# A two-layer hybrid trunk in float32: attention and scan products in fuller rows and in turn, and other work at the two ends

## The chip, the cores and the metric

The kernel runs on one core of a Trainium2 chip. The metric is the device time of one execution in microseconds; the time before is the median of three runs. One more execution was taken with the hardware profiler, and all rows below are from it. The engines are named as in the profile: PE is TensorE (PEld its weight loads), DVE is VectorE, ACT is ScalarE, POOL is GpSimd, and SP issues DMAs.

## The reference

Two layers over 256 tokens of width 2048, in float32. The even layer runs a Mamba-2 scan (SSD, 16 heads of 64) beside block attention (MoBA, 8 heads of 128; at this length each query sees its one block). The odd layer runs NSA (three attention branches, 8 query heads over 2 key heads) beside retention. Each layer then has an output projection, a norm, a gated convolutional FFN and a norm.

```python
def even(h):
    z, xbc, dt, q, k, v = split(h @ w_in)
    y_diag = einsum('bgcls,bghcls,bcsghp->bclghp', cb, decay, xdt_g)   # SSD, one chunk of 256
    o = softmax(q @ k.T * scale + rel_bias, causal) @ v                # MoBA
def odd(h):
    q, kc, vc, ks, vs, kw, vw, gates, rq, rk, rv, rg = split(h @ w_in)
    k_cmp, v_cmp = compress(kc), compress(vc)          # 15 blocks of 32 tokens, stride 16
    o = g0 * attend(q, k_cmp, v_cmp) + g1 * attend(q, ks, vs) + g2 * attend(q, kw, vw)
x = LN(alpha * x + concat(groups) @ w_out)
x = LN(alpha * x + (silu(conv(a)) * u) @ w_down)       # a, u = split(x @ w_up)
```

The relative bias is a table of 32 buckets by 8 heads, spread over distances.

## The kernel before

**Weights.** All weights stream from HBM in slabs of 128 rows. `Weights.prep` (lines 97 to 110) loads a slab into one of four `wraw` buffers, ScalarE rounds it to `whi` (108) and VectorE takes the rest into `wlo` (109); four buffers each. Activations are split in the same way, so that a projection is three fast products per slab: `three` (350 to 355) where the tokens are stationary, and line 314 in `group_b` where the weights are. Products in plain float32 (attention, scan, transposes by a product with the identity) appear in the trace as two records each, transposes as one. SP issues the loads in order; a load waits for its `wraw` buffer, and so for the conversion of four slabs earlier, and that for the products of four slabs earlier.

**Start.** `warm_up` (1151 to 1158) multiplies ones by ones 20 times while the first data arrive. `run` (1160 to 1180) loads x in eight pieces of 256 KB and pumps weight slabs between them, then loads constants and the residual rows `r` (2 MB), and then makes the bias row: `bias_scratch` (558 to 571) multiplies the table by a one-hot matrix (568) and writes the result to DRAM, from where `load_bias` reads it back for each layer. The first group of the even layer (`group_a`, lines 373 to 396) has 16 slabs of 696 columns in two accumulators, the second eight slabs of 688.

**Order.** Small work (SSD, attention, retention) is cut into steps and put into `Fill`; the projection loops pop one step every few products, so that small products stand between large ones. The framework then orders each engine's queue.

**SSD.** `diag(ct)` (839 to 855) makes the output of two heads, each on 64 of 128 columns of the array, with three products a head: first all of one head, then all of the other.

**Attention.** `attn_steps` (599 to 676) gives three steps per head. `scores` multiplies q by k in two parts, as the mask is causal (first 128 queries by 128 keys, the other 128 by 256), into one PSUM tile `S`, then takes the softmax (584 to 593; VectorE adds the bias and takes the minimum, ScalarE the exponential). NSA adds two products with the compressed keys, of 7 and of 15 columns (615, 616). `normalise` scales and transposes by `ident` (639; compressed 652, 653). `mix` (659 to 674) multiplies by the values: per half of the queries and per branch, so three products in MoBA and eight in NSA, of which two have 7 and 15 rows. `pair` puts two heads' steps side by side. `compress` (1002 to 1042) makes the compressed keys and values; its `project` for the values makes two products (1038).

**The last norm.** `out_group` of the last FFN (`idx` 3) finishes the first 128 tokens, then the last six slabs for the other 128; `Norm.start` (194 to 219) then takes mean and variance, GpSimd raises to the power of -0.5 (199), and VectorE makes two passes over each of four column blocks (`first`, `second`) with a store after each. The order there is kept as it is written.

Of the kernel before, what the change touches and what calls it, by code (L numbers as in the profile page):

```python
# [28 lines left out]
WARM = 20  # L29
# [130 lines left out]
class Norm:  # L160
# [33 lines left out]
    def start(self, t):  # L194
# [38 lines left out]
    def store(self, t, at, n):  # L233
        cs = slice(at, at + n)
        self.k.nc.sync.dma_start(self.k.out[128 * t:128 * t + 128, cs], self.k.r[:, t, cs])
# [25 lines left out]
class Trunk:  # L261
# [111 lines left out]
    def group_a(self, act, *evacs, widths=None, early=None):  # L373
# [7 lines left out]
        for s in range(head, KT // m):  # L381
            hi, lo = w.get(first + s)
            for kk in range(m):
                k = m * s + kk
                c = 0
                for n, acc, evac in zip(widths, accs, evacs):
# [171 lines left out]
    def bias_scratch(self):  # L558

        nc = self.nc  # L560
        self.scr = self.dram.tile([8, 384], F32, name="scr")
        with self.tc.tile_pool(name="bias0", bufs=1) as P:
            oh = P.tile([32, 384], F32, name="oh")
            nc.sync.dma_start(oh, self.I["c_onehot"])
            mk = P.tile([8, 384], F32, name="mk")
            nc.sync.dma_start(mk, self.I["c_late"])
            ps = self.ps()
            nc.tensor.matmul(ps[:8, :384], self.rel[:32, :], oh, start=True, stop=True)
            vv = P.tile([8, 384], F32, name="vv")
            nc.vector.scalar_tensor_tensor(vv, ps[:8, :384], -1.0 / SCALE, mk, op0=OP.mult, op1=OP.add)  # L570
            nc.sync.dma_start(self.scr, vv)
# [12 lines left out]
    def softmax(self, P, S, nb0, nb1, w0, w1, z, stat, j):  # L584
# [3 lines left out]
        for i, (c, n, nb) in enumerate(((0, w0, nb0), (w0, w1, nb1))):  # L588
            nc.vector.tensor_tensor_reduce(out=z[:, c:c + n], in0=S[:, c:c + n], in1=nb, scale=SCALE, scalar=3e38,
                                           op0=OP.add, op1=OP.min, accum_out=mn[:, i:i + 1])  # L590
        for i, (c, n) in enumerate(((0, w0), (w0, w1))):
            nc.scalar.activation(z[:, c:c + n], z[:, c:c + n], AF.Exp, scale=-1.0, bias=mn[:, i:i + 1],
                                 accum_out=stat[:, j + i:j + i + 1])
# [5 lines left out]
    def attn_steps(self, P, y, ct, h, branches, gate=None, cmp=None):  # L599
# [4 lines left out]
        ncol = 2 * nbr + (2 if cmp else 0)  # L604

        def scores():
            stat = P.tile([128, 8], F32, name="stat", bufs=4)
            st["stat"], st["z"] = stat, []
            for b, (q, k, _) in enumerate(branches):
                S = self.ps()  # L610
                nc.tensor.matmul(S[:, 0:128], q[:, 0:128], k[:, 0:128], start=True, stop=True)
                nc.tensor.matmul(S[:, 128:384], q[:, 128:256], k, start=True, stop=True)  # L612
                if b == 0 and cmp:
                    kc = cmp[0]
                    nc.tensor.matmul(S[:, 384:391], q[:, 0:128], kc[:, 0:7], start=True, stop=True)
                    nc.tensor.matmul(S[:, 391:406], q[:, 128:256], kc, start=True, stop=True)
                z = P.tile([128, 384], F32, name="z", bufs=self.zbufs)
                self.softmax(P, S, self.nb[:, h, 128:256], self.nb[:, h, :], 128, 256, z, stat, 2 * b)
                st["z"].append(z)
                if b == 0 and cmp:  # L620
                    zc = P.tile([128, 22], F32, name="zc", bufs=4)
                    self.softmax(P, S[:, 384:406], self.nb[:, h, 159:256:16], self.nb[:, h, 31:256:16], 7, 15, zc,
                                 stat, 2 * nbr)
                    st["zc"] = zc

        def normalise():
# [4 lines left out]
            st["pt"] = []  # L631
            for b in range(nbr):
# [634 lines left out]
```

## Time and profile before

| | |
|---|---|
| time, median of 3 runs | 2308.91 us (2308.01 to 2309.33) |
| the profiled execution: time, span | 2309.18 us, 2307.4 us |
| PE busy | 2293.4 us (99%) |
| DVE, ACT, POOL busy | 1418.0, 1105.0, 21.6 us |
| granted PE clock, mean | 0.998 |
| DMA | 436.63 MB, 189 GB/s |

The span runs from the first to the last instruction. Busy PE counts a product from its start to its modelled end, and ends overlap the next start; so what a product costs is read from the distance between starts, or from the chain of waits, where each piece reaches to the next. The chain follows the work that ended last back to the beginning.

### The profile page before, as it was taken

To read this page: it belongs to the slowest core of one execution; us is meant where nothing else is said; L and a number is where in the kernel's file an instruction comes from. 1 tells how busy PE (TensorE), PEld (TensorE's weight loads), DVE (VectorE), ACT (ScalarE), POOL (GpSimd) and SP (SyncE) were. 2 spreads that over 40 slices of the span, in tenths; PEclk is the share of its full clock that TensorE was granted. 3 is DMA by queue.
4 is the path that set the end of the run, shared out by engine and by line. 5 is a ranking of instruction groups with operands and counts; after the bars stand their busy time and mean duration, and the time that the engine had idled before them with its cause. 6 is when DMAs were issued, how large, how long until landed. Compare 5 with 4: busy or idle time off the path is not lost.

```text
span 2307.4 us, 32010 instructions
## 1 busy us (share of the span) xinstructions
PE 2293.4 (99%) x12550; PEld 1981.4 (86%) x12550; DVE 1418.0 (61%) x1921; ACT 1105.0 (48%) x1429; POOL 21.6 (1%) x32
## 2 busy tenths in 40 slices
PE   9999999999999999999999999999999999999998
PEld 9888888888888888888889888889888888888886
DVE  5687667666666665445645667767666666654445
ACT  5555543555555554334345554444545555543332
POOL 0001000000000000000000000000000000000000
PEclk9999999999999999999999999999999999999999
DMA  8664464666666666667557634584666666676664
GB/s 279 199 188 149 162 226 153 202 191 185 190 189 189 189 197 217 193 193 221 176 166 217 212 108 141 167 269 129 192 189 189 190 190 185 190 226 194 193 194 142
DMA packets 128249, 436.63 MB, mean 189 GB/s; under 512 B 14257, under 2 KB 16993, under 8 KB 127713
## 3 DMA queue, kind: packets, MB, share of 16 engines
q1 hardware_dynamic: 128096, 434.58, 60.9%
q8 instruction: 98, 1.61, 0.3%
q14 instruction: 55, 0.44, 0.1%
HBM read 432.41 MB, written 2.11 MB: 188 GB/s over the span
## 4 chain that ended last, share of the span: by engine, by line
PE 98%; DMA 1%; DVE 1%; ACT 0%; issue 0%; SPq 0%; POOL 0%; DVEq 0%; ACTq 0%; POOLq 0%
PE acc L314 57%; PE acc L353 10%; PE acc L355 10%; PE acc L354 10%; PE ps L353 1%; PE ps L354 1%; PE ps L355 1%; PE ps L673 1%; DMA wraw<-in_ev_in 1%; PE acc L338 1%; PE ps L314 0%; PE ps L252 0%; PE ps L612 0%; PE ps L639 0%; PE ps L338 0%; PE acc L345 0%
## 5 line engine op out<-in xcount | busy, mean ns | idle before, releaser
L109 DVE TENSOR_TENSOR wlo<-wraw,whi 128x1024 fp32r<-128x1024 f32 (+4 forms) x794 | 949.2, 1198 | 635.4 <-ACT whi L108 634.2
L314 PE MATMUL acc<-x,whi 128*128 128x512 f32 x3776 | 1178.3, 397 | 0.0
L108 ACT ACTIVATE whi<-wraw 128x1024 fp32r<-128x1024 f32 (+4 forms) x794 | 822.6, 1037 | 728.6 <-PE acc L355 285.8
L314 PEld LDWEIGHTS acc<-x,wlo 128*128 128x128 f32 x3776 | 692.4, 188 | 156.6 <-issue 0.2
L314 PE MATMUL acc<-x,wlo 128*128 128x256 f32 x3776 | 726.1, 279 | 0.0
L314 PEld LDWEIGHTS acc<-x,whi 128*128 128x128 f32 x3776 | 584.3, 189 | 12.5 <-issue 1.2
L353 PE MATMUL acc<-whi,A 128*128 128x512 f32 x448 | 175.9, 393 | 0.0
L405 ACT ACTIVATE tmp<-acc 128x512 f32<-128x512 f32 x120 | 71.8, 598 | 215.5 <-PE acc L314 215.5
L355 PE MATMUL acc<-whi,A 128*128 128x512 f32 x448 | 174.6, 390 | 0.0
L354 PE MATMUL acc<-wlo,A 128*128 128x512 f32 x448 | 174.5, 390 | 0.0
L353 PE MATMUL acc<-whi,B 128*128 128x512 f32 x388 | 150.9, 389 | 0.0
L354 PE MATMUL acc<-wlo,B 128*128 128x512 f32 x388 | 150.9, 389 | 0.0
L355 PE MATMUL acc<-whi,B 128*128 128x512 f32 x388 | 150.9, 389 | 0.0
L355 PEld LDWEIGHTS acc<-whi,A 128*128 128x128 f32 x448 | 84.1, 188 | 17.7 <-DVE A L274 0.3
L353 PEld LDWEIGHTS acc<-whi,A 128*128 128x128 f32 x448 | 84.1, 188 | 17.3 <-ACT A L273 0.4
L354 PEld LDWEIGHTS acc<-wlo,A 128*128 128x128 f32 x448 | 84.2, 188 | 17.0
L353 PE MATMUL acc<-whi,x 128*128 128x512 f32 (+4 forms) x272 | 93.1, 343 | 0.3 <-ACT V L694 0.3
L354 PE MATMUL acc<-wlo,x 128*128 128x512 f32 (+4 forms) x272 | 92.9, 341 | 0.0
L355 PE MATMUL acc<-whi,x 128*128 128x512 f32 (+4 forms) x272 | 92.8, 341 | 0.0
L353 PEld LDWEIGHTS acc<-whi,B 128*128 128x128 f32 x388 | 72.8, 188 | 15.2
L354 PEld LDWEIGHTS acc<-wlo,B 128*128 128x128 f32 x388 | 72.8, 188 | 15.1
L355 PEld LDWEIGHTS acc<-whi,B 128*128 128x128 f32 x388 | 72.8, 188 | 15.0
(289 smaller groups left out, 1619.7 us busy)
## 6 DMA issues: line engine op xcount, KB each, us to landing
wraw<-in_up SPq DMA_DIRECT2D x328, 512.0 KB, 3.9
wraw<-in_down SPq DMA_DIRECT2D x176, 512.0 KB, 4.3
wraw<-in_od_in SPq DMA_DIRECT2D x96, 512.0 KB, 4.2
wraw<-in_ev_in SPq DMA_DIRECT2D x72, 512.0 KB, 3.5
wraw<-in_ev_out SPq DMA_DIRECT2D x32, 512.0 KB, 4.2
wraw<-in_od_out SPq DMA_DIRECT2D x32, 512.0 KB, 4.5
wraw<-in_up SPq DMA_DIRECT2D x32, 384.0 KB, 3.8
wraw<-in_ev_in SPq DMA_DIRECT2D x16, 348.0 KB, 4.5
```

The source lines that it names most:

```text
L108: nc.scalar.activation(hi[:, :n], raw[:, :n], AF.Copy)
L109: nc.vector.tensor_tensor(lo[:, :n], raw[:, :n], hi[:, :n].bitcast(F32), op=OP.subtract)
L314: nc.tensor.matmul(acc, wt, mv, start=(k == 0 and i < len(unit)), stop=(k == nk - 1 and i >= len(unit)))
L338: nc.tensor.matmul(half(acc, t), slabs[k][0][:, 0, c:c + 128], half(act[k], t), start=(k == 0 and t == 0), stop=False)
L353: nc.tensor.matmul(o, xh, wh, start=first, stop=False)
L354: nc.tensor.matmul(o, xh, wl, start=False, stop=False)
L355: nc.tensor.matmul(o, xl, wh, start=False, stop=last)
L405: nc.scalar.activation(t, a[:, :, 256:], AF.Copy, scale=sign)
L673: nc.tensor.matmul(o[:, t * 128:(t + 1) * 128], a, b, start=(i == 0), stop=(i == len(mms) - 1))
```

## The change

- The products on ones at the start are 13 instead of 20. Slabs are pumped two for each piece of x. The first slab of the first group runs its products part by part over both accumulators.
- The bias row's loads are issued behind the first loads of the second group, and its product is put into `Fill` there, nine steps on.
- `diag` runs the two heads in turn.
- NSA: the compressed keys stand ahead of the selected keys in one tile, so that one product makes both scores (144 and 272 columns). The compressed probabilities of two heads share a tile and are transposed together, 32 columns at a time, with the second head. The compressed values are laid out padded with zeros to 128 rows (rows 0 to 15 for the first head of a pair, 16 to 31 for the second), so that one product of 256 columns adds them; the value projection makes four products for this.
- `mix` takes all 256 queries in one product with the first 128 keys and 128 in a second.
- The last norm's second half of the columns: `first` stays on VectorE, TensorE multiplies by a diagonal matrix of the scale (made by ScalarE) on top of the shift (ones by the row of b), ScalarE copies and issues the store. Ahead of it stand 14 products on ones.

On SP's queue, in the first stage: `wraw` is a weight slab, `x_..` the input, `ident`, `prm` and `tri` constants, `r` the residual rows, `oh` and `mk` (after: the two `tmp`) the one-hot matrix and the mask, `scr` the bias row. Before:

```order
L102 DMA wraw<-in_ev_in 128x696 x2
L1171 DMA x_106<-in_x 128x512
L102 DMA wraw<-in_ev_in 128x696 x2
L528 DMA ident<-in_c_ident 128x128
L528 DMA prm<-in_params 128x916
L528 DMA tri<-in_c_tri 128x128
L1175 DMA r<-in_tokens 128x2x2048
L564 DMA oh<-in_c_onehot 32x384
L566 DMA mk<-in_c_late 8x384
L102 DMA wraw<-in_ev_in 128x696
L102 DMA wraw<-in_ev_in 128x688 x2
L571 DMA scr<-vv 8x384
```

And of the change, at the same place:

```order
L1194 DMA x_99<-in_x 128x512
L103 DMA wraw<-in_ev_in 128x696 x2
L551 DMA ident<-in_c_ident 128x128
L551 DMA prm<-in_params 128x916
L551 DMA tri<-in_c_tri 128x128
L1198 DMA r<-in_tokens 128x2x2048
L103 DMA wraw<-in_ev_in 128x688 x3
L587 DMA tmp<-in_c_onehot 32x384
L588 DMA tmp<-in_c_late 8x384
L103 DMA wraw<-in_ev_in 128x688 x5
L103 DMA wraw<-in_ev_in 128x1024 x3
L594 DMA scr<-tmp 8x384
```

The sixteenth slab of 696 columns now stands ahead of the constants and of `r`; the store of the bias row, behind which SP's queue waited for the product, stands eight slabs later.

On PE, one `diag`: `L_..` is the decayed matrix of one head, `xdt` the values. Before:

```order
L846 MATMUL ps_1656<-L_1562,xdt_1253 64x128
L847 MATMUL ps_1656<-L_1562,xdt_1253 64x128
L848 MATMUL ps_1656<-L_1562,xdt_1253 64x128
L846 MATMUL ps_1656<-L_1592,xdt_1253 64x128
L847 MATMUL ps_1656<-L_1592,xdt_1253 64x128
L848 MATMUL ps_1656<-L_1592,xdt_1253 64x128
```

Of the change:

```order
L861 MATMUL ps_1644<-L_1550,xdt_1241 64x128
L861 MATMUL ps_1644<-L_1580,xdt_1241 64x128
L861 MATMUL ps_1644<-L_1550,xdt_1241 64x128
L861 MATMUL ps_1644<-L_1580,xdt_1241 64x128
L861 MATMUL ps_1644<-L_1550,xdt_1241 64x128
L861 MATMUL ps_1644<-L_1580,xdt_1241 64x128
```

The two heads alternate; seven of the eight stand in one piece, and of the last `diag` one product stands apart, where it was three and three.

On PE, the mix of one NSA head, before and of the change (`pt` and `ptc` are transposed probabilities, `vs`, `vw` and `vcmp` values):

```order
L673 MATMUL ps<-pt,vs 128x128
L673 MATMUL ps<-pt,vw 128x128
L673 MATMUL ps<-ptc,vcmp 128x128
L673 MATMUL ps<-pt,vs 128x128 x2
L673 MATMUL ps<-pt,vw 128x128 x2
L673 MATMUL ps<-ptc,vcmp 128x128
```

```order
L687 MATMUL ps<-pt,vs 128x256
L687 MATMUL ps<-pt,vs 128x128
L687 MATMUL ps<-pt,vw 128x256
L687 MATMUL ps<-pt,vw 128x128
L687 MATMUL ps<-ptc_9731,vcmp 128x256
```

Eight products became five, and the one on `ptc` comes last.

```diff
-WARM = 20
+WARM = 13
+WARM_END = 14
...
         if t == 0:
             for c in range(4):
                 self.shift(t, c)
                 self.store(t, 512 * c, 512)
             return
-        self.first(1, 0)
-        self.first(1, 1)
-        self.second(1, 0)
-        self.store(1, 0, 512)
-        self.second(1, 1)
-        self.store(1, 512, 512)
-        self.shift(1, 2)
-        self.store(1, 1024, 512)
-        self.first(1, 3)
+        r = T.r[:, 1, :]
+        accs = [T.ps() for _ in range(2)]
+        for i, acc in enumerate(accs):
+            nc.tensor.matmul(acc, T.ones[0:1, :], self.gb[2 + i][1][0:1, :], start=True, stop=False)
+        spare = T.ps()
+        for _ in range(WARM_END):
+            nc.tensor.matmul(spare[:, :128], T.ones, T.ones, start=True, stop=True)
+        D = T.fpool.tile([128, 2, 256], F32, name="u", bufs=1)[:, 0, :128]
+        self.first(1, 2)
+        self.first(1, 3)
+        nc.scalar.activation(D, T.ident, AF.Copy, scale=rs[:, 1:2])
+        for i, acc in enumerate(accs):
+            c = r[:, 1024 + 512 * i:1536 + 512 * i]
+            nc.tensor.matmul(acc, D, c, start=False, stop=True)
+            nc.scalar.activation(c, acc, AF.Copy)
+            self.store(1, 1024 + 512 * i, 512, nc.scalar)
+        self.shift(1, 0)
+        self.store(1, 0, 512)
+        self.first(1, 1)
         for h in range(2):
-            self.second(1, 3, 256 * h, 256)
-            self.store(1, 1536 + 256 * h, 256)
+            self.second(1, 1, 256 * h, 256)
+            self.store(1, 512 + 256 * h, 256)
...
+                if k == 0 and first == 0:
...
+                    for a, b in ((0, hi), (256, hi), (0, lo)):
+                        for o, t, cs in parts:
+                            nc.tensor.matmul(o, act[0][:, a + t * 128:a + t * 128 + 128], b[:, 0, cs],
+                                             start=(a == 0 and b is hi), stop=False)
...
-    def bias_scratch(self):
+    def bias_scratch(self, P):
...
+        oh, mk = (P.tile([128, 2, 256], F32, name="tmp", bufs=2).rearrange("p a b -> p (a b)")[:, :384]
+                  for _ in range(2))
...
+        self.fill.add(8, go)
...
-                nc.tensor.matmul(S[:, 0:128], q[:, 0:128], k[:, 0:128], start=True, stop=True)
-                nc.tensor.matmul(S[:, 128:384], q[:, 128:256], k, start=True, stop=True)
-                if b == 0 and cmp:
-                    kc = cmp[0]
-                    nc.tensor.matmul(S[:, 384:391], q[:, 0:128], kc[:, 0:7], start=True, stop=True)
-                    nc.tensor.matmul(S[:, 391:406], q[:, 128:256], kc, start=True, stop=True)
+                n = k.shape[1] - 256
+                nc.tensor.matmul(S[:, 0:n + 128], q[:, 0:128], k[:, 0:n + 128], start=True, stop=True)
+                nc.tensor.matmul(S[:, n + 128:2 * n + 384], q[:, 128:256], k, start=True, stop=True)
...
+            if cmp:
+                zc = cmp[1]
+                for t in range(2):
+                    a = zc[:, t, 16 * j:16 * j + 16]
+                    nc.vector.tensor_scalar(a, a, stat[:, 2 * nbr + t:2 * nbr + t + 1], None, op0=OP.mult)
...
+                if cmp and j:
+                    nc.tensor.transpose(pt[:32, 384:512], cmp[1][:, b, :], self.ident)
...
+                if cmp and j:
+                    nc.scalar.activation(cmp[2][:32, 128 * b:128 * b + 128], pt[:32, 384:512], AF.Copy)
...
+            mms = []
+            for (_, _, v), pt in zip(branches, st["pt"]):
+                mms += [(o[:, 0:256], v(0), pt[:, 0:256]), (o[:, 128:256], v(1), pt[:, 256:384])]
+            if cmp:
+                mms.append((o[:, 0:256], cmp[0][:, j, :], cmp[2]))
...
+            self.bias_scratch(P)
             self.group_a(self.xk, ev_v(680))
...
+                for l, t, c, first, last in ((0, 0, 0, True, True), (128, 0, 128, True, False), (128, 1, 256, False, True)):
+                    for j in range(2):
+                        h = 2 * ct + j
+                        nc.tensor.matmul(ps[64 * j:64 * j + 64, l:l + 128], xdt[:, t, 64 * h:64 * h + 64],
+                                         Ls[j][:, c:c + 128], start=first, stop=last)
...
+                kcat = P2.tile([128, 2, 272], F32, name="ks")
...
+                vcmp = P2.tile([128, 2, 2, 128], F32, name="vcmp")
+                zcs = [P2.tile([128, 2, 32], F32, name=f"zc{i}") for i in range(2)]
+                ptcs = [P2.tile([128, 256], F32, name=f"ptc{i}") for i in range(2)]
+                for t in (kcat[:, :, 0:16], *zcs, *ptcs):
+                    nc.gpsimd.memset(t, 0.0)
...
+                nc.vector.memset(pad, 0.0)
+                for j in range(2):
+                    nc.vector.tensor_copy(pad[:, :, j, 16 * j:16 * j + 15], u.rearrange("p (e m) -> p e m", e=2))
                 for e in range(2):
+                    for j in range(2):
+                        c = 256 * e + 128 * j
+                        nc.tensor.matmul(o[:, c:c + 128], pad[:, e, j, :], self.w2[:, 1, :], start=True, stop=True)
...
-                self.w.pump(2 * c + 1)
+                self.w.pump(2 * c + 2)
```

More of the change, by code (lines that the diff above doesn't have):

```diff
@@ L231, in shift, with store @@
         self.second(t, c)
-    def store(self, t, at, n):
+    def store(self, t, at, n, queue=None):
         cs = slice(at, at + n)
-        self.k.nc.sync.dma_start(self.k.out[128 * t:128 * t + 128, cs], self.k.r[:, t, cs])
+        (queue or self.k.nc.sync).dma_start(self.k.out[128 * t:128 * t + 128, cs], self.k.r[:, t, cs])
     def at(self, *where):
@@ L385, in group_a @@
                 c = 0
+                if k == 0 and first == 0:
+                    parts = []
+                    for n, acc in zip(widths, accs):
+                        parts += [(acc[:, t, :n], t, slice(c, c + n)) for t in range(2)]
+                        c += n
+                    for a, b in ((0, hi), (256, hi), (0, lo)):
+                        for o, t, cs in parts:
+                            nc.tensor.matmul(o, act[0][:, a + t * 128:a + t * 128 + 128], b[:, 0, cs],
+                                             start=(a == 0 and b is hi), stop=False)
+                    for _ in widths:
+                        self.fill.pop()
+                    continue
                 for n, acc, evac in zip(widths, accs, evacs):
@@ L582, in load_bias, with softmax @@
             nc.vector.tensor_copy(self.nb[:, 2 * a:2 * a + 2, :], t[:, :, ::-1])
[L584 removed]
+    def softmax(self, P, parts, stat, j):
         nc = self.nc
         mn = P.tile([128, 2], F32, name="mn", bufs=4)
[L588 to L589 removed]
+        for i, (S, nb, z) in enumerate(parts):
+            nc.vector.tensor_tensor_reduce(out=z, in0=S, in1=nb, scale=SCALE, scalar=3e38,
                                            op0=OP.add, op1=OP.min, accum_out=mn[:, i:i + 1])
[L591 to L593 removed]
+        for i, (S, nb, z) in enumerate(parts):
+            nc.scalar.activation(z, z, AF.Exp, scale=-1.0, bias=mn[:, i:i + 1], accum_out=stat[:, j + i:j + i + 1])
     def pair(self, heads, waits=(2, 1, 1)):
@@ L958, in odd @@
                     self.group_b(self.xk, [ev_cmp(i)])
-                for i, n in enumerate(("ks", "kw")):
-                    self.group_b(self.xk, [lambda acc: self.sum_halves(P2, kv[n], acc)])
-                    self.compress(P2, i, *xbs[i], kcmp, vcmp)
+                for i, d in enumerate((kcat[:, :, 16:272], kw)):
+                    self.group_b(self.xk, [lambda acc: self.sum_halves(P2, d, acc)])
+                    self.compress(P2, i, *xbs[i], kcat, vcmp)
                 self.load_bias(P2, P2)
@@ L1015, in compress @@
             if s == 3:
-                rows = P.tile([34, 256], F32, name="crow", bufs=1)
+                rows = P.tile([128, 2, 256], F32, name="k", bufs=2)[:34, 0, :]
                 nc.scalar.activation(rows, acc, AF.Copy)
```

82 lines of the change are left out of this document (24 added, 58 removed).

## The prediction

> **What bounds the kernel.** The page comes first: its chain that ended last tells which engine the time hangs on, and its table of groups how long a copy out of PSUM takes.
>
> ```profile
> PE 98%; DMA 1%; DVE 1%; ACT 0%; issue 0%; SPq 0%; POOL 0%; DVEq 0%; ACTq 0%; POOLq 0%
> ...
> L405 ACT ACTIVATE tmp<-acc 128x512 f32<-128x512 f32 x120 | 71.8, 598 | 215.5 <-PE acc L314 215.5
> ```
>
> TensorE carries 98% of the chain, so a product that goes saves its whole place in the stream, unless another engine then comes late. The 2% that are not TensorE lie at the two ends, and the change touches both. So I read four places: the start, one `diag` of the SSD, one pair of NSA heads, and the tail after the last product. The sum is made against the profiled execution: 2309.18 us, a span of 2307.4 and 1.8 around it. It is 0.27 us over the median of 2308.91.
>
> **The start.** Timeline rows: start, duration, engine, line, operation; in brackets the idle time before and what ended it. The last two are a DMA issue (KB, us to landing) and a row of the windows, which ends with the granted clock, the DMA share and the GB/s.
>
> ```profile
> 5.59 2.29 PE L1158 MATMUL ps<-ones 128*128 128x128 f32 x19
> 7.63 0.41 PE L353 MATMUL acc<-whi,x 128*128 128x352 f32 x1
> 8.58 1.79 DVE L109 TENSOR_TENSOR wlo<-wraw,whi 128x696 fp32r<-128x696 f32 x2 [0.38 <-ACT whi L108]
> 9.61 0.33 PE L353 MATMUL acc<-whi,x 128*128 128x352 f32 x1
> 37.15 0.80 PE L568 MATMUL ps<-oh,prm 32*8 32x384 f32 x2 [1.78 <-DMA wraw<-in_ev_in]
> 37.62 2.46 ACT L108 ACTIVATE whi<-wraw 128x696 fp32r<-128x696 f32 x3 [7.95 <-DMA wraw<-in_ev_in]
> 41.50 0.43 PE L353 MATMUL acc<-whi,x 128*128 128x344 f32 x1 [0.26 <-ACT V L694]
> r<-in_tokens SPq DMA_DIRECT2D x1, 2048.0 KB, 10.5
> ...
> 5.00:10.00 5.00, 5.00 (x39) 5.00 (x38) 3.20 (x5) 3.26 (x5) 0.00 (x0) 1.00 0.98 362
> ```
>
> A float32 product is two records. The last 19 records on ones are 0.11 us apart, so seven products fewer (14 records) bring the first real product from 7.63 to 6.05. The first slab's part ends by 8.0, but the second slab decides: it needs its rounded-off half (line 109), and that half's conversion was the first of the two in the row at 8.58 (0.9 each), so it ended at 9.47. Its DMA now stands ahead of 256 KB of x; at the 362 GB/s of that stretch this is 0.7 us, so 8.75. One slab takes 1.9 to 2.0 (7.63 to 9.61), and TensorE is then some 0.8 us ahead. The stall of 1.78 goes, because the bias product no longer stands there, and so do most of its 0.80; the first group would end near 37.3.
>
> What is late next is the second group's first slab. Its load is queued behind the 2 MB of the residual rows, which took 10.5 us from issue, and now the sixteenth slab (348 KB, 1.0 us at that rate) stands ahead of them too. The row at 37.62 shows three slabs converted back to back once they had landed. I put the conversion of slab 17 (of 24 of the first two groups) at 37.9, and its second half at 39.65; before, the group began at 41.50 and its second product at 41.77. That is 2.1 won, less the bias product, which returns in this group for about 0.9: **1.2 us won**. If that slab lands at 37.0 it is 2.1; if behind everything, at 38.9, it is 0.2. The onehot and mask now use the two `tmp` buffers, which are next written by the first `sum_halves`, some 20 us on: nothing.
>
> **SSD `diag`.** The chain, one of seven `diag` steps in one piece, then half of the eighth:
>
> ```profile
> 207.74 0.36 PE ps L846 x2
> ...
> 208.21 0.06 PE ps L846
> 208.27 0.05 PE ps L847
> ...
> 208.59 0.22 PE ps L848 x2
> 208.81 2.98 PE acc L314 x16
> ...
> 218.54 0.36 PE ps L846 x2
> ...
> 219.34 0.55 PE acc L314 x2
> ```
>
> Twelve records take 1.07 us (207.74 to 208.81), six of one head alone 0.80. In the middle, records of both heads alternate 0.055 apart: the two heads, each on its own 64 columns, already run side by side there. Only the first two and the last two run alone. In turn, ten more records behind the first two would cost 0.36 + 9 x 0.055, or 0.85: 0.22 less. I take 0.2, seven times. The eighth was two separate pieces, 1.60 in all; now one product stands alone and five follow, 0.36 + 0.80. Together **1.8 us**; bounds 0 and 2.2.
>
> By the Trainium skill, "TensorE: Matmul & The Clock Gate", section Part 3, matmuls start and end strictly in program order. The rows disagree: L846 of the second head (208.21) runs ahead of the first head's L848. Were the rule so, nothing would overlap before, a `diag` would stand at 1.6, and this term would be near 6.
>
> **MoBA and NSA.** Again the chain: a MoBA mix, the value projection, then the scores of one head, the transposes of one, and a mix.
>
> ```profile
> 250.28 0.67 PE ps L673 x6
> ...
> 1300.41 0.54 PE ps L1038 x4
> ...
> 1308.47 0.22 PE ps L611 x2
> 1308.69 0.43 PE ps L612 x2
> 1309.13 0.12 PE ps L615 x2
> 1309.25 0.23 PE ps L616 x2
> 1309.48 0.32 PE ps L611 x2
> 1309.80 0.43 PE ps L612 x2
> ...
> 1313.01 0.66 PE ps L639 x6
> 1313.66 0.11 PE ps L652
> 1313.77 0.11 PE ps L653
> 1313.88 1.39 PE acc L314 x8
> ...
> 1318.96 2.36 PE ps L673 x16
> 1321.32 1.59 PE acc L314 x8
> ```
>
> 128 moving columns cost 0.22, 256 cost 0.43; the price goes with the columns.
> - Scores, 1.76 a head. New widths 144 and 272 cost 0.25 and 0.46, with the window's 0.22 and 0.43 (the 0.32 carries 0.10 after the short product): 1.36. Won 0.40, eight heads: 3.2.
> - Transposes: 0.22 a head become two of 0.11 a pair. Four pairs: 0.9.
> - Mix: eight products of 128 should cost 1.78 and take 2.36, and the eight L314 behind take 1.59, not 1.39. Both extras are those of the 7- and 15-row products. Five products over 128 rows cost 3 x 0.43 + 2 x 0.22, or 1.73. Won 0.83, eight times: 6.6.
> - MoBA mix: 0.67 against 0.65, eight times: 0.15.
> - The value projection: four products of 0.22 for 0.54: 0.34 lost. Its memset and two copies on VectorE have `u` some 3 us early: hidden.
>
> New waits. Both heads' compressed columns are transposed with the second head, so the first mix ends on copies by ScalarE that come later. In the first pair a weight conversion (about 1.06 us) stands between the two copies; it frees about when the mix begins, and the fifth product comes 1.30 later: nearly even. And the two scalings of `zc` (about 0.3) now precede those of `z`, while TensorE arrives 0.8 earlier. The `z` of the first head was ready at 1312.3 by the rows below, 0.7 before its transposes.
>
> ```profile
> 1312.10 0.19 ACT L592 ACTIVATION_READ_ACCUMULATOR z<-z,mn 128x1 f32 x1
> 1312.29 0.36 DVE L649 TENSOR_SCALAR zc<-zc,stat 128x7 f32<-128x7 f32 x2
> ```
>
> But its VectorE chain is queued behind the second head's scores, which also come 0.8 earlier, so most of the slack stays. I allow 0.12 a pair, 0.5. NSA and projection: 10.7 - 0.34 - 0.5, **9.9 us**; bounds 6.5 and 10.4.
>
> **The tail.**
>
> ```profile
> 2296.43 0.24 PE ps L355
> ...
> 2299.84 1.41 DVE r L227 x2
> ```
>
> ```profile
> 2298.68 0.98 POOL L199 TENSOR_TENSOR rs<-rs,mhalf 128x1 f32<-128x1 f32 x1 [7.18 <-DVE rs L198]
> 2303.39 0.88 DVE L227 SCALAR_TENSOR_TENSOR r<-r,rs,x 128x256 f32<-128x256 f32 x2
> 2303.90 0.81 SPq L235 DMA_DIRECT2D out_dram<-r  x2
> ```
>
> VectorE loses two passes of 0.70 and would end at 2302.9, not 2304.3: 1.4 won on that path alone. The other path runs over TensorE, and its queue is in order. From 2296.67 two products of one row by 512 columns (four records of 0.43, by width) and 14 on ones (28 of 0.11) take 1.7 + 3.1 + 0.3 for two changes of shape, to 2301.8, though the scaled identity is there by about 2300.0 (the power ends at 2299.66). Two products of 512 end at 2302.8 and 2303.7; ScalarE's copies (0.60) with a DMA issue between end at 2304.4, and the last store is 256 KB where it was 128. Against 2304.3 that is **0.4 us lost**; bounds 0.8 lost (the larger store and a slow issue on ScalarE) and 1.4 won.
>
> **Sum:** 1.2 + 1.8 + 0.15 + 9.9 - 0.4 = 12.65. From 2309.18 that is 2296.5, and by the median, 0.27 lower, **2296.2 us**.
>
> **Rivals.**
> - *The clock falls in the gap at the start.* TensorE would idle from 37.3 to about 39.6, but for one product.
>
> ```profile
> 2299.00:2300.00 1.00, 0.00 (x0) 0.00 (x0) 1.00 (x3) 0.00 (x0) 0.66 (x1) 0.61 0.00 0
> ```
>
>   In this microsecond of the tail the mean clock was 0.61, so it went to a half early in it, some 2.5 us behind the last product. It stayed full over the 1.78 at the start. At the start TensorE ran on ones for some 4.5 us before the first of the 19 records at 5.59, at half their speed; as long a stretch here would lose 2.2: 2298.4. [...]
> - *The softmax chain becomes the bound.* ScalarE's exponentials of a pair end at 1312.29 whatever TensorE does. If that decides, the 0.8 of a pair's scores comes back as waiting, 3.2 in all: 2299.4. Against it: the chain shows no wait there.
> - *The later copies hold the first mix.* If the conversion waits as long again, about 2 us a pair: 8 lost, 2304.
> - *The tail ends on VectorE,* since TensorE's products on ones are done early: 1.8 better, 2294.4.
> - *Other side: taking turns drains the array.* If each change of half costs the 0.2 that follows the 15-row product (1.59 against 1.39), the overlap is gone: a `diag` is six products of 0.22 and six drains, 2.5, or 1.45 more, eight times 11.6. With the 1.8 not won, 2309.6: slower by 0.7 than the median. It decides from a drain of about 0.19. Against it: records of both halves 0.055 apart.
>
> **Chances.** Forecast 0.70; clock 0.07; softmax 0.07; copies 0.05; VectorE tail 0.07; drain 0.04. 0.2% is 4.6 us, about what a measurement tells from no change. Drain, and half of copies with an unlucky start, stay within it: 0.06; slower by more needs drain and copies at once: 0.01. Faster: 0.93. The range takes all terms at their good bounds, and the bad side to 2302.5, which takes in clock and softmax together: 2292.5 to 2302.5.
>
> **What would show it.** Start: no wait before the bias product; the second group's first products near 39.6, waiting for a slab's conversion; clock 1.0 there. SSD: a `diag` of 0.85 to 0.9 from its first record to the next L314. NSA: a mix of 1.73 with 1.39 behind it, scores of 1.36, no TensorE wait for ScalarE or VectorE from 1300 to 1400. Tail: products on ones running past the scaled identity, and the last store from ScalarE. The forecast is wrong if the mix still takes over 2 us, if TensorE waits in the odd layer, or if the gap at the start grows past 3 us.

## The result, and the profile after

| | before | after |
|---|---|---|
| time, median (range, 4 runs each) | 2308.91 us (2308.01 to 2309.33) | 2296.24 us (2295.52 to 2299.37) |
| ratio to before, with 95% interval | | 0.9948 (0.9936 to 0.9961) |
| the profiled execution: time, span | 2309.18, 2307.4 us | 2295.52, 2293.7 us |
| granted PE clock, mean | 0.998 | 1.000 |

The change made the kernel 12.7 us faster by the medians; 2296.2 was predicted. The lines of the changed file differ: 353 to 355 are now 364 to 366, 314 is 325, 109 is 110, 846 to 848 are 861, 611 and 612 are 637 and 638, 673 is 687. A stage's gain is read as the difference of the same mark in the two chains: how much earlier the first projection product behind a stage starts than before, less what it was ahead already.

| stage | predicted | measured |
|---|---|---|
| start, to the first L314 (L325) | 1.2 | 56.91 to 55.44: 1.47 |
| SSD, to the first score of MoBA | 1.8 | 238.51 to 234.61: 2.4 more |
| MoBA, to its last mix | 0.15 | 307.51 to 303.42: 0.2 more |
| value projection and NSA, to retention's first product | 9.9 | 1405.69 to 1391.48: 10.1 more |
| tail, last projected product to the end | -0.4 | 10.73 to 11.21: -0.48 |

The timeline of after around the end of the first group, as in the prediction (start, duration, engine, line; in brackets the idle time before and what ended it):

```profile
36.91 0.73 ACT L708 ACTIVATE V<-acc 128x672 f32<-128x672 f32 x1 [6.18 <-DVE dt L706]
37.54 0.77 ACT L109 ACTIVATE whi<-wraw 128x688 fp32r<-128x688 f32 x1
38.34 0.88 DVE L110 TENSOR_TENSOR wlo<-wraw,whi 128x688 fp32r<-128x688 f32 x1 [1.52 <-ACT whi L109]
38.36 0.42 PE L364 MATMUL acc<-whi,x 128*128 128x344 f32 x1 [0.83 <-ACT whi L109]
39.27 0.42 PE L365 MATMUL acc<-wlo,x 128*128 128x344 f32 x1 [0.49 <-DVE wlo L110]
```

The wait ahead of the bias product is gone; the second group waits for slab 17 and its second product starts at 39.27 (forecast 39.65; 41.77 before). The first conversion of that slab stands behind an evacuation on ScalarE, which looks like a second cause beside the slab's landing. That is tested below.

The chain of after, with two `diag` steps, the value projection, the scores of one head, the mixes of the first pair, and the tail:

```profile
162.05 0.81 PE ps L861 x12
162.86 2.98 PE acc L325 x16
...
215.06 0.36 PE ps L861 x2
215.42 1.01 PE acc L325 x4
216.43 0.80 PE ps L861 x10
...
1296.27 0.89 PE ps L1062 x8
1297.16 4.20 PE acc L325 x24
1301.36 0.24 PE ps L637 x2
1301.60 0.46 PE ps L638 x2
1302.06 0.22 PE ps L637 x2
1302.28 0.43 PE ps L638 x2
...
1313.98 1.88 PE ps L687 x10
1315.87 1.40 PE acc L325 x8
1317.27 1.74 PE ps L687 x10
...
2282.49 1.91 PE ps L212 x4
2284.40 3.32 PE ps L215 x28
2287.72 0.88 PE ps L222 x2
...
2288.62 0.61 ACT r L223
```

A `diag` takes 0.81 (1.07 before), scores 1.35 a head (1.76), a mix 1.74 with 1.40 behind it (2.36 and 1.59). The first mix takes 0.14 more: its last product starts at 1315.20, just behind ScalarE's second copy of compressed probabilities, which ends at 1315.05. It is the only mix of the eight that shows this wait. The tail ends on ScalarE's copies, behind 28 records on ones, as forecast.

### The profile page after: what moved, and what is told of

It reads as the page before. It is cut to its first block, busy times and chain, and to the rows that moved or that the text cites. A ratio compares the mean times of both kernels' runs of the same rounds, so it can differ in the third digit from the quotient of the medians.

```text
span 2293.7 us, 31859 instructions
## 1 busy us (share of the span) xinstructions
PE 2286.9 (100%) x12472; PEld 1974.7 (86%) x12472; DVE 1417.6 (62%) x1922; ACT 1105.2 (48%) x1424; POOL 22.0 (1%) x37
## 3 DMA queue, kind: packets, MB, share of 16 engines
q8 instruction: 97, 1.59, 0.3%
## 4 chain that ended last, share of the span: by engine, by line
PE 99%; DVE 0%; ACT 0%; issue 0%; POOL 0%; ACTq 0%; POOLq 0%
PE acc L325 57%; PE acc L366 11%; PE acc L365 11%; PE acc L364 11%; PE ps L366 1%; PE ps L365 1%; PE ps L364 1%; PE ps L687 1%; PE acc L349 1%; PE ps L325 0%; PE ps L263 0%; PE ps L638 0%; PE ps L667 0%; PE acc L356 0%; PE ps L349 0%; PE ps L861 0%
## 5 line engine op out<-in xcount | busy, mean ns | idle before, releaser
L325 PE MATMUL acc<-x,whi 128*128 128x512 f32 x3776 | 1178.9, 398 | 0.0
L325 PEld LDWEIGHTS acc<-x,wlo 128*128 128x128 f32 x3776 | 692.4, 188 | 156.0 <-issue 0.2
L325 PE MATMUL acc<-x,wlo 128*128 128x256 f32 x3776 | 726.4, 279 | 0.0
L325 PEld LDWEIGHTS acc<-x,whi 128*128 128x128 f32 x3776 | 585.0, 189 | 11.7 <-issue 1.4
```

Of the source, the lines that this page charges most:

```text
L325: nc.tensor.matmul(acc, wt, mv, start=(k == 0 and i < len(unit)), stop=(k == nk - 1 and i >= len(unit)))
```

## The experiments

Each of these kernels was profiled in one execution; where rounds of timing were made, the median is given. They ran on four chips, on which the kernel before took 2308.15 to 2309.12.

### The start: what holds the second group

Two edits, each alone. In the first a dependence puts the conversion of slab 17 (`conv`) ahead of the evacuation on ScalarE:

```diff
-                nc.scalar.activation(V[:, :, 0:336], acc[:, :, 16:352], AF.Copy)
+                act = nc.scalar.activation(V[:, :, 0:336], acc[:, :, 16:352], AF.Copy)
+                self.tc.add_manual_dep(act.ins, self.w.conv, mybir.DependencyInfo(
+                    mybir.DependencyClass.NoSync, mybir.DependencyReason.DATA), reason="conversion first")
```

> The changed kernel, with the conversion of slab 17 (the second group's first) put ahead of the first evacuation into V on ScalarE; in the changed kernel it starts at 37.54, behind that evacuation, and the second group's first product with the rounded-off half (L365) at 39.27. Theory A, the slab's landing decides and ScalarE's order adds a little: its load was issued at 26.4 and landed 10.5 later, at 36.9, so the conversion starts at 36.9 to 37.3 and L365 at 38.6 to 39.0, 0.3 to 0.6 won. Rival B, landing alone: L365 stays at 39.2 to 39.3. Rival C, ScalarE's order alone: the slab had landed long before, the conversion moves to about 33 to 35 and the second group follows the first at once, L365 by 37.2, 2 won.

In the second the residual rows move:

```diff
-        nc.sync.dma_start(self.r, self.I["tokens"].rearrange("(t p) c -> p t c", t=2))
...
                 for i in range(4):
+                    nc.sync.dma_start(self.r[:, :, 512 * i:512 * i + 512],
+                                      self.I["tokens"][:, 512 * i:512 * i + 512].rearrange("(t p) c -> p t c", t=2))
                     self.group_b(self.xk, [ev_xbc(xs[:, 2 * i:2 * i + 2, :], 2 * i, i)])
```

> The changed kernel with the 2 MB of residual rows loaded later, in four pieces ahead of the last four groups of the convolved stage, so that the second group's slabs are not queued behind them. Theory A (the residual rows hold slab 17): it lands by about 31, and the second group follows the first within 0.3: L364 near 36.7, first L314 of the next stage 2.0 to 2.4 earlier than 55.44, that is 53.0 to 53.5, and the whole 2 lower. Rival C (ScalarE's order alone): the same start as in the changed kernel if the order stays. Rival D: the pieces cost as much where they stand now, and later marks come back to those of the changed kernel (scores of k and q at 234.4).

Timeline of ScalarE and TensorE with the conversion first, then two rows of its windows (length, busy time of PE, PEld, DVE, ACT and POOL, granted clock, DMA share, GB/s):

```profile
39.84 0.78 ACT L109 ACTIVATE whi<-wraw 128x688 fp32r<-128x688 f32 x1 [9.70 <-DMA wraw<-in_ev_in]
40.52 0.71 ACT L710 ACTIVATE V<-acc 128x672 f32<-128x672 f32 x1
41.29 0.65 PE L366 MATMUL acc<-whi,x 128*128 128x344 f32 x1 [4.32 <-ACT V L710]
```

```profile
39.00:40.00 1.00, 0.00 (x0) 0.00 (x0) 0.00 (x0) 0.16 (x1) 0.00 (x0) 0.85 0.53 185
40.00:41.00 1.00, 0.00 (x0) 0.00 (x0) 0.35 (x1) 1.00 (x2) 0.00 (x0) 0.50 0.15 61
```

And from ScalarE's timeline with the residual rows later:

```profile
31.62 0.78 ACT L109 ACTIVATE whi<-wraw 128x688 fp32r<-128x688 f32 x1 [1.64 <-DMA wraw<-in_ev_in]
```

With the conversion first, ScalarE sat idle for 9.70 and was released by the slab's landing, at 39.84 in this execution: rival C falls. None of the three forecast times came, since the slab landed 2 to 3 later than in the profile of after, where the rows in front of it were also issued 1.7 earlier (25.84; here 27.58); so what ScalarE's order is worth (at most the 0.6 by which the evacuation precedes it) was not measured. TensorE idled 4.32, and the clock fell at 39.7 and came back at 46.5 (windows 0.85, then 0.50 up to 0.74 in 46 to 47); the first L325-type product came at 59.79. With the rows later the slab is converted at 31.62, TensorE's timeline shows no wait between 36 and 44, the next stage starts at 52.75 instead of 55.27 (the timeline's mark), and the whole takes 2292.71, 2.8 under the profiled execution of after. The gain stays: the first score of MoBA comes 2.5 earlier than in after (232.13 against 234.61), so rival D falls. Theory A holds: the 2 MB hold the second group after the change. Of the kernel before only the trace says the same (ScalarE waits 7.95 for the slab behind the rows); the rows were not moved there.

### Which part of the change won at the start

> The changed kernel with slabs pumped as before, one more than twice the piece of x, so that the sixteenth slab again stands behind the residual rows. Theory A (the place of the sixteenth slab in SP's queue is what the change won at the start): that slab lands at about 37, the first group's last products wait for it from 34.7, and the second group's first L314-stage mark comes at 57.0 to 58.0 instead of 55.44: 1.6 to 2.5 lost. Rival E (the later bias product is what won it): under 0.5 lost, 55.4 to 55.9.

```diff
-                self.w.pump(2 * c + 2)
+                self.w.pump(2 * c + 1)
```

The next two are the kernel before with one part of the change each: the bias row, and the products on ones with the first slab's order (the new hunk of `group_a`).

```diff
-        self.bias_scratch()
...
+            self.bias_scratch(P)
             self.group_a(self.xk, ev_v(680))
```

> The kernel before, with only the bias row's loads and product moved as in the change. The prediction's step (the stall of 1.78 and the 0.80 of the product go): the first L314 comes 1.0 to 2.5 earlier than 56.74, 54.2 to 55.7. Theory P (the slab behind the residual rows decides, the product stood in that wait, and only the two small loads ahead of the slab counted): the slab lands 0.2 to 1.0 earlier, and the product returns later for 0.74: 56.0 to 57.2, between 0.7 won and 0.5 lost.

```diff
-WARM = 20
+WARM = 13
...
+                if k == 0 and first == 0:
```

> The kernel before, with only the 13 products on ones and the first slab part by part over both accumulators. Theory Q (the loads wait for buffers, the buffers for products: an earlier first product brings the issue of the residual rows and all behind them forward): their issue moves from 25.92 to 24.8 to 25.2, and the first L314 from 56.74 to 55.6 to 56.1. Rival R (the queues are full and pace themselves): 56.3 to 57.0.

The starts of these and other kernels, by their timelines:

| kernel | first conversion behind the residual rows | first product of the next stage | low clock |
|---|---|---|---|
| before | 37.62 | 56.74 | no |
| before, mix padded (below) | 37.14 | 56.26 | no |
| before, bias row later | 36.29 | 56.33 | no |
| before, 13 products on ones, first slab in parts | 36.26 | 56.38 | no |
| after, sixteenth slab behind the rows | 35.33 | 55.36 | no |
| after | 37.54 | 55.27 | no |
| after, 7 products on ones at the end | 36.99 | 56.26 | 39.2 to 42.6 |
| after, conversion first | 39.84 | 59.79 | 39.7 to 46.5 |
| after, residual rows later | 31.62 | 52.75 | no |

(Where the sixteenth slab stands behind the rows, the first conversion is that slab's, else slab 17's.) Four more profiles with after's start put its mark at 55.06 to 55.27, without a low clock. The sixteenth slab's place is worth nothing (theory A of that run fell): ahead of the rows it delays them (their load was issued at 25.84 with it and at 24.63 without), behind them it waits itself; as a whole that kernel took 2295.59. The bias row alone won 0.41 and the start of the first group alone 0.36, both by less than the 0.48 between the two executions with the start unchanged. Theory P holds for the size of the first; for the second, the rows' issue moved only from 25.92 to 25.54, and the mark landed in neither theory's way clearly (Q 55.6 to 56.1, R 56.3 to 57.0: R by a little). One reason why the second alone gives so little shows on VectorE; timelines of the kernel with the earlier first slab, and of the one with the bias row later:

```profile
37.62 0.55 DVE L582 SCALAR_TENSOR_TENSOR vv<-ps,mk 8x384 f32<-8x384 f32 x1 [6.68 <-PE ps L580]
38.09 1.65 DVE L109 TENSOR_TENSOR wlo<-wraw,whi 128x696 fp32r<-128x696 f32 x2
```

```profile
37.10 1.71 DVE L109 TENSOR_TENSOR wlo<-wraw,whi 128x696 fp32r<-128x696 f32 x2 [6.08 <-ACT whi L108]
```

Both slabs were converted from 36.3 on. With the bias row in its old place its scaling stands ahead of the slab's second half on VectorE, and the half starts 1.0 later; with the row later that 1.0 is won, and the product returns for 0.74. As wholes the two took 2308.82 and 2308.84, the kernel before beside them 2308.65. The two edits together are the start of the kernel with the sixteenth slab behind the rows, and there they won 1.38 (56.74 to 55.36), more than the 0.77 of the two alone. Why they win more together was not shown beyond this order on VectorE; the rows were also issued earlier there (24.63; 25.21 and 25.54 with one edit).

### The clock in the gap

The kernel with 7 products on ones at the end differs from after in the tail alone, so its start is one more execution of after's. TensorE's timeline and windows at the start:

```profile
37.81 0.42 PE L364 MATMUL acc<-whi,x 128*128 128x344 f32 x1 [1.17 <-ACT whi L109]
38.72 0.43 PE L365 MATMUL acc<-wlo,x 128*128 128x344 f32 x1 [0.48 <-DVE wlo L110]
```

```profile
38.00:39.00 1.00, 0.52 (x3) 0.28 (x3) 0.67 (x1) 1.00 (x3) 0.00 (x0) 1.00 0.08 31
39.00:40.00 1.00, 1.00 (x6) 1.00 (x6) 0.91 (x2) 0.91 (x3) 0.00 (x0) 0.58 0.32 41
```

Its second group's second product began earlier than after's (38.72 against 39.27), and yet the clock fell at 39.2 and the next stage came 1.0 later: 1.54 lost behind that product. TensorE had idled 1.17 and 0.48 there, 0.83 and 0.49 in after; but in two others of the same start it idled as long (1.21 and 0.48, the kernel with the old SSD order; 1.22 and 0.48, the one with products of one row below) and the clock stayed at 1.00. So idle time of 1.65 us in all at this place costs nothing in some executions and 1.5 in another. The Trainium skill ("TensorE: Matmul & The Clock Gate", Part 1) has a window that runs freely, by which the same gap can fall either way. But it asks for an idle window of about 3.4 us, and here the clock fell after 1.65 us of idling, and in the tail of before at 2299.2, 2.55 behind the last product; on that point the measurement decides.

> The changed kernel itself, on the same chip as the kernel with the later rows and the other tail, for the ratio of the two. Theory N (with the residual rows ahead of slab 17 each execution has a gap of 2 to 4 at the start, and in some of them the clock falls in it): the executions spread over 2 to 5, between 2295.3 and 2300, and the slow ones have a mean clock of 0.998 or 0.999; the kernel without that gap spreads over under 1. Rival: both spread alike.

After was timed five more times beside the best kernel: 2295.49 to 2298.29, median 2295.80, and only the execution of 2298.29 had a mean clock of 0.999; among the first four it was that of 2299.37 with 0.998. That fits theory N, though no profile of those two exists to show the place. Its second half failed: the kernel without the gap still spreads over 1.88 (below), so the gap isn't the only source.

### SSD

After with the old order, all of one head first:

```diff
-                for l, t, c, first, last in ((0, 0, 0, True, True), (128, 0, 128, True, False), (128, 1, 256, False, True)):
...
+                    nc.tensor.matmul(o[:, 0:128], xh[0], L[:, 0:128], start=True, stop=True)
+                    nc.tensor.matmul(o[:, 128:256], xh[0], L[:, 128:256], start=True, stop=False)
+                    nc.tensor.matmul(o[:, 128:256], xh[1], L[:, 256:384], start=False, stop=True)
```

> The changed kernel with the SSD diag products in the old order, all of one head, then all of the other. Theory (the ends of each run stood alone): each diag takes 1.07 from its first record to the next L314 instead of 0.81, the eighth 1.60 instead of 1.16, and the scores of k and q behind the stage come 2.2 to 2.5 later than 234.4. Rival (taking turns costs at the changes of half): the old order is even or faster, later by under 0.5.

The first score of MoBA came at 237.04 instead of 234.61, with the same first L325 (55.27) in both; the whole took 2297.96. Its chain has the old pieces back, 1.07 for a whole `diag` (162.05 to 163.12) and 0.80 and 0.80 for the eighth. So taking turns wins 2.4, and the rival, that each change of half drains the array, is out. The pieces of the chain account for 2.3 of it (seven times 0.265, and 0.44).

### NSA

In the kernel before, only the padding; its main lines:

```diff
-                vcmp = P2.tile([15, 2, 128], F32, name="vcmp")
+                vcmp = P2.tile([128, 2, 128], F32, name="vcmp")
+                ptcs = [P2.tile([128, 256], F32, name=f"ptc{i}") for i in range(2)]
+                for t in (vcmp, *ptcs):
+                    nc.gpsimd.memset(t, 0.0)
...
-                    n = 7 if t == 0 else 15
-                    mms.append((cmp[1][:n, :], st["ptc"][:n, t * 128:(t + 1) * 128]))
+                    mms.append((cmp[1], st["ptc"][:, t * 128:(t + 1) * 128]))
```

> The kernel before, with only the compressed probabilities and values padded with zeros to 128 rows; each mix still has eight products of 128 columns. Theory H (the 7- and 15-row products cost extra, in the mix and behind it): a mix takes 1.75 to 1.80 instead of 2.36 and the eight L314 behind it 1.39 to 1.41 instead of 1.59, 6.0 to 6.4 won in all, nearly all of what the changed kernel wins in the mix (2.36 to 1.74). Rival I (fewer and wider products are what wins): the mix stays above 2.2 and the eight L314 behind it at 1.59, under 1.5 won.

Its chain, the first pair's mixes:

```profile
1318.47 1.79 PE ps L672 x16
1320.26 1.40 PE acc L314 x8
1321.66 1.79 PE ps L672 x16
```

Theory H holds. The eight products are all still there, with as many columns, and take 1.79 with 1.40 behind, where two of them with 7 and 15 rows made it 2.36 and 1.59. That is 0.76 of the 0.81 that the change wins for a mix and what follows; fewer and wider products add 0.05. The kernel took 2302.98, 5.9 under the kernel before on the same chip.

By a table in "TensorE: Matmul & The Clock Gate" of the Trainium skill (section "Why this matters for your kernels") a single product over 32 rows takes as long as one over 128; by that alone padding would be worth nothing. For products of 7 and 15 rows amid products of 128 rows these rows say otherwise.

### The tail

Fewer products on ones, 7 (as below) and none:

> The changed kernel with 7 products on ones at the end instead of 14. Theory F: these products, not the scaled identity, set TensorE's part of the tail; 14 records of 0.119 go, and the last product ends 1.66 earlier. Then VectorE's path ends last (last pass ended at 2288.84, 6.35 behind the last projected product), and from the last L366-type product to the span's end it takes 9.4 to 9.7 instead of 11.21: 1.5 to 1.8 won. Rival G: the clock or the stores set the end, and under 0.5 is won.

> The changed kernel without products on ones at the end. Theory F (they hide nothing here): TensorE idles about 1.5 (from 1.9 behind the last projected product until the scaled identity at 3.43 behind it), too short for the clock to fall, and the end is VectorE's: 9.4 to 9.7 from the last projected product to the span's end, 1.5 to 1.8 won, as with 7. Rival G (they keep the clock): the two products by the scaled identity run at half speed, about 0.85 longer each, and the end comes within 0.5 of the changed kernel's 11.21, or the granted clock shows a fall there.

```diff
-WARM_END = 14
+WARM_END = 7
```

Over several executions the tail is best measured from the start of VectorE's last statistics to the span's end: 9.94 to 9.98 in the four profiles with before's tail; 10.45, 10.46, 10.49, 10.52 and 10.22 in five with after's; 9.60 with 7 products on ones, 10.43 with none. So 14 lose 0.24 to 0.58, and with 7 the tail is 0.85 shorter than after's: half of what theory F gives. As wholes the two took 2295.58 (the one with 7, which had the low clock at its start) and 2295.31. Windows of the kernel with 7, the last but one column the DMA share:

```profile
2289.00:2290.00 1.00, 0.00 (x0) 0.00 (x0) 0.79 (x2) 0.60 (x1) 0.00 (x0) 1.00 0.91 346
2290.00:2291.00 1.00, 0.00 (x0) 0.00 (x0) 0.00 (x0) 0.00 (x0) 0.00 (x0) 1.00 1.04 353
2291.00:2292.00 1.00, 0.00 (x0) 0.00 (x0) 0.00 (x0) 0.00 (x0) 0.00 (x0) 0.98 0.95 339
```

VectorE's last pass ended at 2289.79, ScalarE's last copy at 2289.73, but the DMA engines are full from 2289 to 2292: the 1 MB of the last 128 tokens takes 3 us at 350 GB/s, and these stores end the kernel, 1.8 behind their last bytes. In after the share was 0.56, 0.87 and 0.68 from 2289 to 2292. Neither the prediction nor theory F had counted the stores against one another. With no products on ones, timeline and windows:

```profile
2282.24 1.98 PE L212 MATMUL ps<-x,ones 1*128 1x512 f32 x4
2285.79 3.78 PE L222 MATMUL ps<-r,u 128*128 128x512 f32 x4 [1.58 <-ACT u L219]
```

```profile
2284.00:2285.00 1.00, 0.22 (x1) 0.00 (x0) 0.96 (x4) 0.00 (x0) 0.68 (x1) 0.72 0.00 0
2285.00:2286.00 1.00, 0.21 (x1) 0.21 (x2) 1.00 (x2) 0.40 (x1) 0.30 (x1) 0.50 0.00 0
```

Rival G: the two products by the scaled identity take 3.78 instead of 1.88, the clock at a half. It fell at 2284.44, 2.1 behind the last product of 128 rows, though TensorE was busy until 2284.22, with four products of one row. In the kernel with the conversion first it fell at 2289.08, 2.0 behind the last projected product: the four products of one row had just run, and those on ones had started 0.15 before. Their 28 records took 5.02:

```profile
2287.01 1.98 PE L214 MATMUL ps<-x,ones 1*128 1x512 f32 x4
2288.93 5.02 PE L217 MATMUL ps<-ones 128*128 128x128 f32 x28
```

That made its tail 12.16 and, with the 4.5 at its start, the whole of its 6.2 over after. Do products of one row not count for the clock? All 14 with one row:

```diff
-            nc.tensor.matmul(spare[:, :128], T.ones, T.ones, start=True, stop=True)
+            nc.tensor.matmul(spare[:, :128], T.ones[0:1, :], T.ones[0:1, :], start=True, stop=True)
```

> The changed kernel, whose 14 products on ones at the end use one row of the ones instead of 128, so that from the last projected product to the scaled identity TensorE runs only products of one row. Theory S (products of one row do not hold the clock: it fell 2.0 behind the last product of 128 rows in one run and 2.2 in another, while or just after four products of one row ran): the granted clock falls to a half 1.9 to 2.7 behind the last projected product, the products on ones take about 5 to 6.5 instead of 3.3, the two by the scaled identity 3.8 instead of 1.9, and the tail is 3 to 5 longer. Rival T (any product holds the clock; the falls came from where the clock's window lay): the granted clock stays 1.00 until the last product, and the tail stays at 10.9 to 11.3 from that product to the span's end.

```profile
2285.04 3.40 PE L215 MATMUL ps<-ones 1*128 1x128 f32 x28
2288.38 3.51 PE L222 MATMUL ps<-r,u 128*128 128x512 f32 x4
```

```profile
2287.00:2288.00 1.00, 1.00 (x11) 1.00 (x11) 0.90 (x3) 0.00 (x0) 0.00 (x0) 1.00 0.00 0
2288.00:2289.00 1.00, 1.00 (x4) 0.65 (x4) 0.96 (x3) 0.00 (x0) 0.00 (x0) 0.53 0.05 20
```

TensorE was busy without a break, and the clock fell at 2288.06, while these products ran: they don't hold it here. But it fell 4.8 behind the last product of 128 rows (2283.29), not 1.9 to 2.7, and the products on ones, still at the full clock, took 3.40. So theory S is right in kind and wrong in time. The tail is 1.5 longer than after's (2283.22 to 2296.0 against 2282.42 to 2293.7); the rest of the 2.3 by which this execution (2297.78) lies over after's was lost ahead of the tail, between the marks 1508.7 and 1543.8 of VectorE's statistics (1508.8 and 1543.0 in after). There its chain runs over late loads of weight slabs, where that of after stays on TensorE, so this loss has nothing to do with the edit at the end.

### A version that beats both

The later residual rows, 6 products on ones, and VectorE's order at the end changed:

```diff
         self.first(1, 2)
-        self.first(1, 3)
+        self.first(1, 0)
         nc.scalar.activation(D, T.ident, AF.Copy, scale=rs[:, 1:2])
+        self.second(1, 0)
+        self.store(1, 0, 512)
+        self.first(1, 3)
...
-        self.shift(1, 0)
-        self.store(1, 0, 512)
         self.first(1, 1)
```

> The changed kernel with the residual rows loaded later, in four pieces, as in the run that did only that, and another tail: 6 products on ones instead of 14, and VectorE finishes the first quarter of the columns (both passes and its store) between the first passes of the third and of the fourth quarter. Theory L (at the end 1 MB has to be stored, and the stores already filled the queues where there were 7 products on ones; so the first store has to start earlier): the first store is issued about 4.0 behind the last projected product instead of 4.8, and from there the 1 MB at 360 GB/s, a start of 1.0 and a close of 1.5 give 9.4 to 9.8 from that product to the span's end, against 11.21 in the changed kernel. With the 2.5 of the start: 2291.0 to 2291.8 in all. Rival G (the clock falls at the end with so few products on ones): 10.5 or more for the tail, 2292.5 or more in all. Rival M (the stores are bound by VectorE's last pass alone): no better than the 10.35 of the run with 7.

2293.25 median of 5 (2292.07 to 2293.95), ratio to before 0.9931 (0.9919 to 0.9944). After took 2295.80 beside it (0.9946, 0.9933 to 0.9960); the executions of the two don't overlap, though the intervals do. The forecast of 2291.0 to 2291.8 was too good by 1.5. In its profile (2292.07) the tail takes 10.2 from the last projected product, not 9.4 to 9.8: TensorE waits 0.22 for the fourth quarter's first pass, and its last copy starts at 2286.07. The first store was issued at 2284.22, 4.1 behind that product as forecast, but the tail is only 0.15 shorter than the 10.35 of the run with 7, so rival M is not clearly out. The DMA engines were no longer full (a share of 0.68, 0.74 and 0.92 from 2285 to 2288), since the last store had to wait for the last copy.

```profile
2284.91 1.12 PE L225 MATMUL ps<-r,u 128*128 128x512 f32 x2 [0.22 <-DVE r L235]
2286.07 0.60 ACT L226 ACTIVATE r<-ps 128x512 f32<-128x512 f32 x1 [0.75 <-PE ps L225]
```

Of the executions at the median, 1.2 longer, there is no profile. The later rows alone took 2292.71 in their one execution, within the range of this kernel; so the times don't show what its tail adds. By the profiles it is 0.76: 9.46 from VectorE's last statistics to the end against 10.22.

## Why the prediction was right

The steps named what bounds each stage, and each stage came within 0.7 of its term. That the time lies within 0.1 us of the median is luck: the stages of the two profiled executions add up to 13.7, against the 12.65 of the sum, since start, SSD and NSA were each put too low, while the profiled execution of after was 0.7 faster than the median of its kernel. By the steps:

- **Start, 1.2 against 1.47.** The cause was named rightly: the second group's first slab is held by the 2 MB of residual rows, which the run with the rows later shows. Two steps to the number were not right. The stall of 1.78 and most of the 0.80 were to go: with the bias row moved alone only 0.41 went; TensorE still waited 0.20 and 0.33 for the slab behind the rows, and the product came back for 0.74. And the seven products on ones were to bring the first slab forward: alone, with the slab in parts, 0.36. Both together won 1.38, which no step had as such. The forecast held because what was late next had been worked out by itself, as a time at which slab 17 is ready.
- **The clock in that gap, given 0.07.** It did not happen in the profile of after, but in one of the six profiles that have its start, the one with 7 products on ones at the end, at a price of 1.5 (2.2 forecast), and in one with another order on ScalarE. So the chance looks too small, though one in six is no proof of it. The median doesn't show it; the slowest executions may.
- **SSD, 1.8 against 2.4.** Mechanism right, shown by undoing it. A `diag` took 0.81 where 0.85 was forecast, and the upper bound of 2.2 was too low by 0.2.
- **NSA, 9.9 against 10.1.** The two extras put down to the 7- and 15-row products are shown by padding alone: 0.57 in the mix and 0.19 behind it. Scores, transposes and mixes came within 0.02 each; those of scores and transposes are read from the chains, not tried apart. The 0.5 for new waits was too much: 0.14 in the first mix, and some 0.2 in the fourth pair, where the chain passes over VectorE. The value projection cost 0.35, but the 24 products behind it took 0.18 less (4.20, 4.38 before), which the step had not counted.
- **Tail, 0.4 lost against 0.48.** It ends on ScalarE's copies as worked out. That VectorE's path would otherwise end the kernel 1.4 earlier than before, or 1.8 earlier than forecast, as step and rival had it, is wrong: with 7 products on ones it was 0.4 against before and 0.85 against after, and there the stores of 1 MB are the bound.
- The rivals of the softmax chain and of the drained array did not occur: chain and `diag` show neither.

## What to carry to other kernels

A wait that shows in front of an instruction is not won by moving that instruction; work out when the next thing in the same queue is ready, here a slab behind 2 MB that are first used some 280 us later, and move what fills the queue. Products over few rows can cost more than the same columns over 128 rows, in themselves and in what follows, so padding with zeros may win without any other change. At the end of a kernel count the stores as a stage of their own: once the engines are quick enough, the bytes of the last tile over the DMA rate can set the end. An earlier first store helps only if the last one comes early too: here it won 0.15.

## What was not expected of the hardware

- Products of one row did not hold TensorE's clock: in one execution it fell while they ran, 4.8 us after the last product of 128 rows, and in two others just behind four of them, 2.0 and 2.1 us after it. The products on ones at the end with 128 rows kept it at 1.00 in seven of the eight profiles that have them; in the eighth the clock fell 0.15 after they had begun.
- About the same idle time, 1.65 to 1.70 us in two parts, in front of the second group left the clock at 1.00 in two executions and halved it for 3.4 us in a third.
- A product over 7 or 15 rows amid products of 128 rows made a mix 0.57 longer and the eight products behind it 0.19.
